# A float32 transformer block on one core: seven products for eight in the output projection's first two strips and in gate and up groups 0, 9 and 10, and the fourth merged quarter transposed by block exchange

## The chip, the core and the metric

The kernel runs on one core of a Trainium2 chip. The metric is the device time of one execution in microseconds. The core's engines are TensorE (PE, matmuls), VectorE (DVE), ScalarE (ACT), GpSimd (POOL) and SyncE (SP, which only issues DMAs); each works through its own instructions in a fixed order and waits where it needs another's result.

## The reference

One transformer block on 256 rows of 2048 numbers in float32. Three mixers (sparse attention, state space, retention) read one input projection; their outputs are merged, and what this case is about follows:

```python
    merged = g_nsa * (y_nsa @ p_nsa) + g_ssd * (y_ssd @ p_ssd) + g_ret * (y_ret @ p_ret)
    return merged @ w_out
...
    x = x + mix.astype(x.dtype)
    f = rms_norm(x, norm_ffn[l])
    x = x + ((jax.nn.silu(f @ w_gate[l]) * (f @ w_up[l])) @ w_down[l]).astype(x.dtype)
return rms_norm(x, norm_final)
```

`w_out` is 2048 x 2048, `w_gate` and `w_up` are 2048 x 5632, `w_down` is 5632 x 2048.

## The kernel before

**A product.** Each float32 number is split into a high part (fp32r, made by ACT: `wh`, `mh`, `fh`) and the rest (made by DVE as number minus high part: `wl`, `ml`, `fl`). A product of a 128x128 block of activations with a 128x512 block of weights is three matmuls into one PSUM bank: high x high, high x low, low x high. The 256 rows are two row tiles t. Activations are kept transposed, features on partitions, in 16 blocks of 128 (`mh`, `ml` for merged, `fh`, `fl` for the normalized x2); four blocks are a quarter.

**stream()** multiplies by one strip of 512 weight columns. For each pair of feature blocks it loads a 512 KB tile `raw` (SP's queue), makes `wh` and `wl` of it (rings of four), and issues four products, 12 matmuls. **stream_pair()** takes two strips at once, in eight steps j of two feature blocks each. A plain j is 8 products, 24 matmuls, into four banks c11 to c22. A fast j adds and subtracts blocks of the weights on DVE, needs ready-made sums of activation blocks (X, from `block_sums()`), and does 7 products, 21 matmuls, some into the four further banks m1, m5, m6, m7, which `capture()` adds into the result at the end of the last fast j. Which j are fast, and the order of the steps, are lists given by the caller.

**The stages around the change.** `merge_pair()` makes the two halves of merged. Its quarters 0, 1 and 2 are transposed into `mh`, `ml` by `task_exchange()`: DVE transposes 32x32 blocks into `tq`, 16 DMAs on POOL's queue move them to `st_x`, ACT makes the high part, DVE the low one. There is one `st_x` buffer at a time, so an exchange's DMAs wait until the one before has been read. Quarter 3 goes through 8 PE transposes into banks `hv` instead. Then four strips of `w_out` follow in stream(); `ev_o` adds half of each to x2, which `open_x2()` has loaded with x by four POOL DMAs. Behind each strip `task_f` transposes that quarter of x2 into `fh`, `fl` (quarters f0, f1, f2 by exchange with four scalings, f3 by 8 PE transposes `tf`). Then come 11 groups of one gate and one up strip, each a stream_pair. In groups 1 to 8 j=0 and 1 are fast, groups 0, 9 and 10 are plain. During them x2 lies in DRAM (`res`), its space holding sums and raw tiles; four POOL DMAs bring it back before group 10. The down projection adds the last product.

**What sets the order.** Tasks are generators in queues (`urgent` and others), of which a step is taken every third matmul; a queue is emptied at fixed places (`drain`). From that a scheduler makes each engine's order, with a high priority for weight loads and splits. A POOL DMA waits for the DMA eight before it on the queue.

Of the kernel before, what the change touches and what calls it, by code (L numbers as in the profile page):

```python
# [121 lines left out]
def _build(tc, a):  # L122
# [45 lines left out]
    def aux(name="ax"):  # L168
        return xp.tile([P, 512], F32, tag="ax", name=name)
# [48 lines left out]
    def pause(n):  # L218
        for _ in range(n):
            yield  # L220
# [43 lines left out]

    def stream_pair(xh, xl, K, srcs, cps, mps, order, X, capture, evac, new_raw, new_half, fast, hooks={}, tail=0):
        names = ("c11", "c12", "c21", "c22")
        C = [cps.tile([P, 512], F32, tag="mp" if cps is mp else "ax", name=n) for n in names]
        M = [mps.tile([P, 512], F32, tag="mp" if mps is mp else "ax", name=n) for n in ("m1", "m5", "m6", "m7")] if fast else []  # L270
# [43 lines left out]
        for n, j in enumerate(order[:len(order) - tail]):  # L314
            with tc.high_priority(offset=3000):
                ra, rb = load(j, 0), load(j, 1)
                h1, l1 = tiles()
                if j in fast:
                    wsum(rb[:, 0], rb[:, 0], rb[:, 1])
                halves(h1, l1, ra)  # L320
                if j in fast:
                    wsum(ra[:, 0], ra[:, 0], rb[:, 0])
                    wsum(ra[:, 1], ra[:, 1], ra[:, 0])
                    h2, l2 = new_half()
                    halves(h2, l2, rb[:, 1])
# [24 lines left out]
            if n in hooks:  # L350
                hooks[n]()
            if n == len(order) - 4:
                drain(urgent)
        for c in range(2 if tail else 0):
            held = []
# [832 lines left out]
    ml = mtp.tile([P, KD, S], F32R, name="ml")  # L1188

    def task_merged(c):  # L1190
        if c < 3:
            yield from pause(2)
            yield from task_exchange(mtp, merged[:, :, c * 512:(c + 1) * 512], mh, ml, c * 4)
            return
        yield from pause(6)
        for t in range(NT):
            ps = aux("hv")
            for b in range(4):
                transpose(ps[:, b * P:(b + 1) * P], merged[:, t, (4 * c + b) * P:(4 * c + b + 1) * P])
                yield  # L1200
            pv = ps.rearrange("p (b q) -> p b q", b=4)
            o = (slice(None), slice(4 * c, 4 * c + 4), slice(t * P, (t + 1) * P))
            act(mh[o], pv, AF.Copy)
            V.tensor_tensor(ml[o], pv, mh[o], OP.subtract)

    for c in (0, 2):
        merge_pair(2, yrh, yrl, 8, a["p_ret"], c, lambda c: urgent.append(task_merged(c)))
# [27 lines left out]
    for c in range(4):
        cs = slice(c * 512, (c + 1) * 512)

        def ev_o(t, ps):
            if c == 0 and t == 0:
                open_x2()  # L1240
            x2 = box["x2"]
            V.scalar_tensor_tensor(x2[:, t, cs], ps, 0.5, x2[:, t, cs], OP.mult, OP.add)
            jk = box["tmp"].tile([P, 512], F32, tag="jk", name="jk", bufs=3)
            act(jk, x2[:, t, cs], AF.Square, accum_out=sq2[:, t, c:c + 1])
        stream(mh, ml, KD, a["w_out"], c * 512, 512, ev_o)
# [26 lines left out]
    flip = [0]  # L1272

    def group(i):
        fast = GF if 1 <= i <= 8 else []
        if i == 9:
            s9_es.close()
            late, box["late_es"] = pool("late")
            for x_, n in ((hh, "hh9"), (hl, "hl9")):
                x_.late = late.tile([P, 4, S], F32R, name=n)  # L1280
        hb = tmp_p.tile([P, NT, 512], F32, tag="hb", name="hb", bufs=2)
        src = {}

# [110 lines left out]
    for c in (0, 2):  # L1394
        def capture(m1, m5, m6, m7):
            x = [[x2[:, t, (c + n) * 512:(c + n + 1) * 512] for n in range(2)] for t in range(NT)]
            u, f = (tmp_p.tile([P, 512], F32, tag="jk", name=n, bufs=3) for n in ("u", "m5s"))
            act(u, m1, AF.Copy)
            act(f, m5, AF.Copy)
            V.tensor_tensor(x[0][0], x[0][0], m1, OP.add)  # L1400
            V.tensor_tensor(u, u, m6, OP.add)
            V.tensor_tensor(x[0][1], x[0][1], f, OP.add)
            V.tensor_tensor(x[0][1], x[0][1], u, OP.subtract)
            V.tensor_tensor(u, u, m7, OP.add)
            V.tensor_tensor(x[1][0], x[1][0], u, OP.add)
# [9 lines left out]
        order = spread(4, std, fast, 4) if c == 0 else spread(1, std, fast, 3)  # L1415
# [34 lines left out]
```

## Time and profile before

| | |
|---|---|
| median of 3 runs (lowest, highest) | 1791.72 us (1791.63, 1792.75) |
| the profiled execution: its time, its span | 1790.73 us, 1789.0 us |
| TensorE busy | 1775.5 us, 99% |
| VectorE, ScalarE, GpSimd busy | 73%, 51%, 14% |
| chain that ended last | PE 96%, issue 2%, DVE 1% |

The span is what the profiler saw between the first and the last instruction; the execution's own time is 1.73 us longer. "Busy" of PE counts pipelined matmuls, so 99% means that it seldom waits.

### The profile page before, as it was taken

How to read it: one execution, taken by the hardware profiler on the slowest of the kernel's cores; microseconds unless marked ns; L12 is line 12 of the kernel's file. 1: busy time of each engine (PE TensorE's matmuls, PEld its weight loads, DVE VectorE, ACT ScalarE, POOL GpSimd, SP SyncE). 2: the span in 40 equal slices, each digit the busy share in tenths (PEclk: the TensorE clock that was granted, in tenths of full speed). 3: DMA queues.
4: the chain of work that ended last, by engine and by line, in shares of the span. 5: the costliest groups of instructions: out<-in, count | busy, mean ns of one | idle time of the engine just before them, and what ended most of it. 6: DMA issues, size and time to landing. Idle time of an engine off the chain costs nothing.

```text
span 1789.0 us, 22765 instructions
## 1 busy us (share of the span) xinstructions
PE 1775.5 (99%) x8220; PEld 1476.3 (83%) x8220; DVE 1304.8 (73%) x1613; ACT 920.6 (51%) x1170; POOL 242.6 (14%) x447
## 2 busy tenths in 40 slices
PE   9999999999999999999999999999999999999997
PEld 8878888988888888888888788888888888888886
DVE  7698986656664446577777665989998885777876
ACT  7465554546554444445445444555555554454543
POOL 0002222000000001310132430111112221100000
PEclk9999999999999999999999999999999999999999
DMA  9366555864555654656566886666666676676663
GB/s 354 118 213 200 188 169 162 264 201 153 162 166 166 200 186 156 221 191 212 186 202 214 267 262 224 199 222 212 204 210 203 206 241 209 200 228 211 198 211 118
DMA packets 196993, 362.52 MB, mean 203 GB/s; under 512 B 17056, under 2 KB 31648, under 8 KB 196368
## 3 DMA queue, kind: packets, MB, share of 16 engines
q1 hardware_dynamic: 181760, 335.65, 58.6%
q0 software_dynamic: 14688, 24.72, 4.1%
q8 instruction: 64, 1.05, 0.2%
q10 hardware_dynamic: 432, 0.70, 0.1%
q14 instruction: 49, 0.40, 0.1%
HBM read 344.71 MB, written 4.23 MB: 195 GB/s over the span
## 4 chain that ended last, share of the span: by engine, by line
PE 96%; issue 2%; DVE 1%; DMA 0%; ACT 0%; POOL 0%; POOLq 0%; DVEq 0%; ACTq 0%
PE mp L251 42%; PE c L288 41%; PE m L288 5%; PE hp L589 3%; PE yd L737 1%; PE c L859 0%; DMA erow<-adram 0%; PE pT L193 0%; DVE erow L696 0%; PE hp L564 0%; PE ny L811 0%; PE ny L807 0%; PE ny L809 0%; PE yo L742 0%; DVE wl L239 0%
## 5 line engine op out<-in xcount | busy, mean ns | idle before, releaser
L155 ACT ACTIVATE wh<-raw 128x1024 fp32r<-128x1024 f32 (+2 forms) x568 | 593.1, 1048 | 606.2 <-PE mp L251 305.4
L239 DVE TENSOR_TENSOR wl<-raw,wh 128x1024 fp32r<-128x1024 f32 (+2 forms) x304 | 365.9, 1207 | 227.5 <-ACT wh L155 224.5
L300 DVE TENSOR_TENSOR wl<-raw,wh 128x1024 fp32r<-128x1024 f32 x264 | 321.4, 1225 | 140.2 <-ACT wh L155 135.9
L251 PE MATMUL mp<-wl,uh 128*128 128x512 f32 (+2 forms) x832 | 319.1, 384 | 1.5 <-DVE wl L239 1.5
L251 PE MATMUL mp<-wh,ul 128*128 128x512 f32 (+2 forms) x832 | 319.7, 385 | 0.0
L251 PE MATMUL mp<-wh,uh 128*128 128x512 f32 (+2 forms) x832 | 317.8, 391 | 0.0
L449 POOL DMA_DIRECT2D st_x<-tq x368 | 182.6, 503 | 459.1 <-DVE tq L446 396.3
L288 PE MATMUL c<-wl,fh 128*128 128x512 f32 x608 | 236.7, 389 | 0.0
L288 PE MATMUL c<-wh,fl 128*128 128x512 f32 x608 | 236.5, 389 | 0.0
L288 PE MATMUL c<-wh,fh 128*128 128x512 f32 x608 | 226.4, 390 | 0.0
L251 PEld LDWEIGHTS mp<-wh,ul 128*128 128x128 f32 x832 | 156.4, 188 | 29.9 <-issue 0.2
L251 PEld LDWEIGHTS mp<-wh,uh 128*128 128x128 f32 x832 | 155.6, 188 | 30.6
L251 PEld LDWEIGHTS mp<-wl,uh 128*128 128x128 f32 x832 | 156.6, 188 | 29.1 <-DVE wl L239 1.9
L155 ACT ACTIVATE wh<-x 128x1024 fp32r<-128x1024 f32 x80 | 84.8, 1060 | 122.5 <-PE c L288 65.4
L288 PEld LDWEIGHTS c<-wh,fh 128*128 128x128 f32 x608 | 114.0, 188 | 24.2 <-ACT wh L155 0.4
L288 PEld LDWEIGHTS c<-wl,fh 128*128 128x128 f32 x608 | 114.1, 188 | 23.8 <-DVE wl L300 0.4
L288 PEld LDWEIGHTS c<-wh,fl 128*128 128x128 f32 x608 | 114.1, 188 | 23.7
L300 DVE TENSOR_TENSOR wl<-x,wh 128x1024 fp32r<-128x1024 f32 x80 | 97.5, 1219 | 23.1 <-ACT wh L155 23.0
L288 PE MATMUL c<-wl,hh 128*128 128x512 f32 x292 | 113.6, 389 | 0.0
L288 PE MATMUL c<-wh,hl 128*128 128x512 f32 x292 | 113.6, 389 | 0.0
L288 PE MATMUL c<-wh,hh 128*128 128x512 f32 x292 | 108.1, 389 | 0.0
L288 PEld LDWEIGHTS c<-wh,hh 128*128 128x128 f32 x292 | 54.8, 188 | 11.4
(423 smaller groups left out, 2611.7 us busy)
## 6 DMA issues: line engine op xcount, KB each, us to landing
raw<-in_w_in_dram SPq DMA_DIRECT2D x240, 512.0 KB, 3.6
raw<-in_w_up_dram SPq DMA_DIRECT2D x88, 512.0 KB, 4.7
raw<-in_w_down_dram SPq DMA_DIRECT2D x88, 512.0 KB, 4.9
x<-in_w_gate_dram SPq DMA_DIRECT2D x64, 512.0 KB, 4.5
raw<-in_p_ssd_dram SPq DMA_DIRECT2D x32, 512.0 KB, 3.7
raw<-in_w_out_dram SPq DMA_DIRECT2D x32, 512.0 KB, 4.6
raw<-in_w_gate_dram SPq DMA_DIRECT2D x24, 512.0 KB, 4.5
st_x<-tq POOLq DMA_DIRECT2D x368, 32.0 KB, 3.8
```

The source lines that it names most:

```text
L155: return nc.scalar.activation(out, in_, func, **kw)
L239: V.tensor_tensor(wl[:, ks, :n], raw[:, ks, :n], wh[:, ks, :n], OP.subtract)
L251: mm = nc.tensor.matmul(o, xx[:, k, ts], ww[:, kk, :n], start=(k == 0 and i == 0), stop=(k == K - 1 and i == 2))
L288: mm = nc.tensor.matmul(bank[o], xx, ww, start=first and i == 0, stop=last and i == 2)
L300: behind("DVE", V.tensor_tensor(o, u, v, op))
L449: queue.dma_start(st[32 * b:32 * b + 32, x], tq[32 * x:32 * x + 32, b])
L589: nc.tensor.matmul(hps[c][t][:, 0:n], xx[:, k, ts], ww[:, c0:c0 + n], start=(k == 0 and i == 0), stop=(k == KD - 1 and i == 2))
L737: nc.tensor.matmul(ps[:, h * 64:(h + 1) * 64], erow[:, h, t, :], xdt[:, t, h * 64:(h + 1) * 64], start=True, stop=True)
```

## The change

1. The output projection's first two strips become one stream_pair with j=0 and 1 fast, in the order 2, 3, 0, 4, 5, 1, 6, 7. The activation sums XO are made by block_sums. `capture_o` adds half of the m banks straight into x2. x2 is loaded (`open_x2`) behind the fourth step. Strips 2 and 3 stay with stream(), in the other four banks. The f tasks of quarters 0 and 1 are both queued behind the pair.
2. Groups 0, 9 and 10 have j=0 and 1 fast too. Group 0 goes 2, 3, 4, 0, 5, 1, 6, 7 and makes the sums of `fh`, `fl` that group 1 made. Groups 9 and 10 use parts of x2's space for sums and raw tiles.
3. The fourth merged quarter goes through task_exchange like the others.
4. x2 comes back from DRAM behind group 10, not before it. The down projection's first pair spreads its fast steps by `spread(6, ...)`, not 4.

```diff
     def task_merged(c):
-        if c < 3:
-            yield from pause(2)
-            yield from task_exchange(mtp, merged[:, :, c * 512:(c + 1) * 512], mh, ml, c * 4)
-            return
-        yield from pause(6)
-        for t in range(NT):
-            ps = aux("hv")
-            for b in range(4):
-                transpose(ps[:, b * P:(b + 1) * P], merged[:, t, (4 * c + b) * P:(4 * c + b + 1) * P])
-                yield
...
-            act(mh[o], pv, AF.Copy)
-            V.tensor_tensor(ml[o], pv, mh[o], OP.subtract)
+        yield from pause(2)
+        yield from task_exchange(mtp, merged[:, :, c * 512:(c + 1) * 512], mh, ml, c * 4)
...
+    def half_more(x, v, s_=0.5):
+        V.scalar_tensor_tensor(x, v, s_, x, OP.mult, OP.add)
+
+    def capture_o(m1, m5, m6, m7):
+        x = [[box["x2"][:, t, n * 512:(n + 1) * 512] for n in range(2)] for t in range(NT)]
+        u, f = (box["tmp"].tile([P, 512], F32, tag="jk", name=n, bufs=3) for n in ("uo", "m5o"))
+        act(u, m1, AF.Copy)
+        act(f, m5, AF.Copy)
+        half_more(x[0][0], m1)
+        V.tensor_tensor(u, u, m6, OP.add)
+        half_more(x[0][1], f)
+        half_more(x[0][1], u, -0.5)
+        V.tensor_tensor(u, u, m7, OP.add)
+        half_more(x[1][0], u)
+        half_more(x[1][1], f)
+        half_more(x[1][1], u, -0.5)
+
+    XO = block_sums(mh, ml, 0, 2, mg["left"], *xs)
+    stream_pair(mh, ml, KD, [(a["w_out"], 0), (a["w_out"], 512)], mp, xp, [2, 3, 0, 4, 5, 1, 6, 7], XO, capture_o,
...
+                {3: open_x2}, drains=(2, 4))
+    for c in range(2):
+        urgent.append(task_f(c))
+    for c in range(2, 4):
+        stream(mh, ml, KD, a["w_out"], c * 512, 512, lambda t, ps: ev_o(c, t, ps), banks=xp)
         urgent.append(task_f(c))
...
     def group(i):
-        fast = GF if 1 <= i <= 8 else []
+        fast = GF
+        parts = sums if i < 9 else [x2[:, 0, n * 512:(n + 1) * 512] for n in range(4)]
...
         def half():
+            if i > 8:
+                return [hlp.tile([P, 2, 512], F32R, tag=t, name=t)[:, 0] for t in ("wh", "wl")]
...
-        order = std[:2] + fast[:1] + std[2:4] + fast[1:] + std[4:]
-        if i == 1:
+        order = std[:2] + fast[:1] + std[2:4] + fast[1:] + std[4:] if i else [2, 3, 4, 0, 5, 1, 6, 7]
+        if i == 0:
...
             XG.update(block_sums(fh, fl, 0, len(GF), tmp_p, *v))
```

On POOL's queue, around the output projection, the order was this before: the last addition into merged, the loads of x2 (`x2<-in_x_dram`), and then a write of one quarter of x2 to DRAM (`res`) ahead of each f quarter's sixteen exchange DMAs.

```order
L1076 TENSOR_TENSOR merged_2620<-merged_2620,gt_7813 128x512 x2
L1223 DMA x2_8516<-in_x_dram 128x2x512 x4
L1322 DMA res_9085<-x2_8516 256x1x512
L449 DMA st_x_8548<-tq_8547 32x256 x16
L1322 DMA res_9085<-x2_8516 256x1x512
L449 DMA st_x_8726<-tq_8725 32x256 x16
L1322 DMA res_9085<-x2_8516 256x1x512
L449 DMA st_x_8904<-tq_8903 32x256 x16
L1322 DMA res_9085<-x2_8516 256x1x512
```

And the same stretch of POOL's queue in the changed kernel:

```order
L1076 TENSOR_TENSOR merged_2620<-merged_2620,gt_7813 128x512 x2
L1211 DMA x2_8563<-in_x_dram 128x2x512 x4
L449 DMA st_x_8404<-tq_8403 32x256 x16
L1331 DMA res_9151<-x2_8563 256x1x512
L449 DMA st_x_8766<-tq_8765 32x256 x16
L1331 DMA res_9151<-x2_8563 256x1x512
L449 DMA st_x_8891<-tq_8890 32x256 x16
L1331 DMA res_9151<-x2_8563 256x1x512 x2
L449 DMA st_x_8970<-tq_8969 32x256 x16
```

The merged quarter's exchange (`st_x_8404`) now stands behind the loads of x2, and f2's exchange (`st_x_8970`) behind all four `res` writes, where it had three ahead of it.

On DVE, before, the third and the fourth merged quarter's low parts stood together in the first output strip, behind that strip's weight splits:

```order
L239 TENSOR_TENSOR wl_8476<-raw_8474,wh_8475 128x1024
L239 TENSOR_TENSOR wl_8494<-raw_8492,wh_8493 128x1024
L466 TENSOR_TENSOR ml_7299<-st_x_8264,mh_7298 128x4x8x32
L1204 TENSOR_TENSOR ml_7299<-hv_8385,mh_7298 128x4x128
L1204 TENSOR_TENSOR ml_7299<-hv_8410,mh_7298 128x4x128
```

In the changed kernel the fourth quarter's low part is this row on DVE, the last one, near the end of the output pair:

```order
L300 TENSOR_TENSOR wl_8705<-raw_8700,wh_8704 128x1024
L300 TENSOR_TENSOR wl_8709<-raw_8702,wh_8708 128x1024
L1230 SCALAR_TENSOR_TENSOR x2_8563<-m5o_8653,x2_8563 128x512 x2
L1230 SCALAR_TENSOR_TENSOR x2_8563<-uo_8652,x2_8563 128x512
L1241 TENSOR_TENSOR uo_8652<-uo_8652,m7_8381 128x512
L1230 SCALAR_TENSOR_TENSOR x2_8563<-uo_8652,x2_8563 128x512 x2
L466 TENSOR_TENSOR ml_7299<-st_x_8404,mh_7298 128x4x8x32
```

It has moved behind the last weight splits of the pair and behind six operations of `capture_o`.

On DVE in group 0 of the changed kernel, the scaling of f2 (L464) stands behind the block sums (`bs`, `hl` by L402) and the first fast step's weight sums:

```order
L411 TENSOR_TENSOR bs_9170<-bs_9170,bs_9171 128x256
L300 TENSOR_TENSOR raw_9311<-raw_9311 128x512
L300 TENSOR_TENSOR hl_9143<-raw_9313,hh_9142 128x512
L402 TENSOR_TENSOR hl_9143<-bs_9170,hh_9142 128x2x128
L300 TENSOR_TENSOR raw_9313<-raw_9311,raw_9313 128x512
L300 TENSOR_TENSOR wl_9326<-raw_9311,wh_9325 128x1024
L1259 TENSOR_SCALAR r2_8349<-r2_8349 128x2
L1260 TENSOR_TENSOR r2_8349<-r2_8349 128x2
L464 TENSOR_SCALAR st_x_8970<-st_x_8970,prm_76 128x4x64 x4
L466 TENSOR_TENSOR fl_8347<-st_x_8970,fh_8346 128x4x8x32
```

Before, that scaling was the fourth row behind the last output strip's additions to x2, with two weight splits of group 0 and none of the sums ahead of it.

On PE the fast step of group 0 meets f2 here (`wh_9279` is of step 4, whose activations are quarter f2):

```order
L288 MATMUL m1_9181<-wl_9316,fh_8346 128x512
L288 MATMUL m1_9181<-wh_9315,fl_8347 128x512
L288 MATMUL m6_9183<-wh_9325,hh_9142 128x512
L288 MATMUL m6_9183<-wl_9326,hh_9142 128x512
L288 MATMUL m6_9183<-wh_9325,hl_9143 128x512
L288 MATMUL c11_9177<-wh_9279,fh_8346 128x512
L288 MATMUL c11_9177<-wl_9280,fh_8346 128x512
L288 MATMUL c21_9179<-wh_9279,fh_8346 128x512
```

Before, step 4 was the fifth of the group; now it is the third, with one m1 and one m6 product of step 0 ahead of it.

## Rows read from the trace of the kernel before

**Rows 1.** The page's parts 1 and 4: busy time and the chain.

```profile
PE 1775.5 (99%) x8220; PEld 1476.3 (83%) x8220; DVE 1304.8 (73%) x1613; ACT 920.6 (51%) x1170; POOL 242.6 (14%) x447
...
PE 96%; issue 2%; DVE 1%; DMA 0%; ACT 0%; POOL 0%; POOLq 0%; DVEq 0%; ACTq 0%
```

**Rows 2.** The waits of PE, whole span: us in total, times, longest.

```profile
PE mp L251 <- DVE wl L239: 1.5, 1, 1.5
...
PE mp L251 <- ACT mh L155: 1.2, 1, 1.2
PE mp L251 <- DVE ml L466: 0.2, 1, 0.2
```

**Rows 3.** The chain that ended last, groups 2 and 3: start, us, what.

```profile
1181.16 10.43 PE c L288 x46
...
1196.35 21.76 PE c L288 x96
...
1223.32 10.43 PE c L288 x46
```

**Rows 4.** Stretches: length, busy us of PE, PEld, DVE, ACT, POOL; clock; DMA share; GB/s.

```profile
950.00:1000.00 50.00, 49.75 (x224) 41.08 (x222) 35.69 (x35) 25.41 (x28) 15.48 (x24) 1.00 0.67 213
1000.00:1050.00 50.00, 48.78 (x214) 40.06 (x215) 30.46 (x34) 23.22 (x29) 19.42 (x37) 1.00 0.85 277
1150.00:1200.00 50.00, 50.00 (x220) 40.95 (x219) 46.04 (x52) 29.12 (x33) 7.84 (x16) 1.00 0.70 224
1500.00:1550.00 50.00, 50.00 (x222) 41.40 (x221) 30.61 (x32) 23.20 (x24) 7.88 (x16) 1.00 0.65 205
1780.00:1785.00 5.00, 0.00 (x0) 0.00 (x0) 2.44 (x7) 1.63 (x5) 0.54 (x1) 0.85 0.86 286
```

**Rows 5.** PE's timeline around the hv transposes: start, us, operation, idle before.

```profile
998.72 1.03 PE L193 MATMUL hv<-cst,merged 128*128 128x128 f32 x8
1000.97 0.50 PE L251 MATMUL mp<-wh,mh 128*128 128x512 f32 x1 [1.22 <-ACT mh L155]
...
1002.42 0.74 PE L251 MATMUL mp<-wh,ml 128*128 128x512 f32 x2 [0.25 <-DVE ml L466]
```

**Rows 6.** DVE's timeline in group 1.

```profile
1133.15 0.69 DVE L300 TENSOR_TENSOR raw<-x,raw 128x512 f32<-128x512 f32 x1
1133.76 1.22 DVE L300 TENSOR_TENSOR wl<-x,wh 128x1024 fp32r<-128x1024 f32 x1
1134.89 0.42 DVE L411 TENSOR_TENSOR bs<-bs 128x256 f32<-128x256 f32 x1
1135.23 0.42 DVE L402 TENSOR_TENSOR hl<-bs,hh 128x256 fp32r<-128x256 f32 x1
```

**Rows 7.** POOL's timeline, the loads of x2.

```profile
1000.35 2.92 POOL L1223 DMA_DIRECT2D x<-in_x_dram  x4 [6.44 <-issue]
```

**Rows 8.** DMA issues from 1000 to 1003.5 us: count, size, median us to landing.

```profile
x<-in_x_dram POOLq DMA_DIRECT2D x4, 512.0 KB, 9.4
```

**Rows 9.** Tile st_x, whole span: DMA issue to landing.

```profile
DMA to landing us min/median/max: 1.6/3.8/6.9
```

**Rows 10.** Groups of instructions by form, 990 to 1160 us: xcount | busy us, mean ns.

```profile
L464 DVE TENSOR_SCALAR st_x<-st_x,prm 128x256 f32<-128x256 f32 x12 | 3.5, 347 | 0.2 <-issue 0.2
L155 ACT ACTIVATE fh<-st_x 128x1024 fp32r<-128x1024 f32 x3 | 3.2, 1056 | 0.4 <-DMA res<-x 0.4
```

**Rows 11.** POOL's timeline, exchanges of f1 and f2 and the last res write.

```profile
1039.57 4.43 POOL L449 DMA_DIRECT2D st_x<-tq  x9 [2.74 <-DVE fl L466]
...
1048.70 2.02 POOL L449 DMA_DIRECT2D st_x<-tq  x4 [0.38 <-DMA st_x<-tq]
...
1063.07 5.43 POOL L449 DMA_DIRECT2D st_x<-tq  x11 [5.01 <-DVE fl L466]
...
1070.64 1.48 POOL L449 DMA_DIRECT2D st_x<-tq  x3 [0.17 <-issue]
1079.12 0.71 POOL L1322 DMA_DIRECT2D res<-x  x1 [7.00 <-DVE x L1242]
```

More of the change, by code (lines that the diff above doesn't have):

```diff
@@ L263, in stream, with stream_pair @@
             evac(t, ps[t][:, :n])
-    def stream_pair(xh, xl, K, srcs, cps, mps, order, X, capture, evac, new_raw, new_half, fast, hooks={}, tail=0):
+    def stream_pair(xh, xl, K, srcs, cps, mps, order, X, capture, evac, new_raw, new_half, fast, hooks={}, tail=0, drains=()):
         names = ("c11", "c12", "c21", "c22")
@@ L351, in stream_pair @@
                 hooks[n]()
-            if n == len(order) - 4:
+            if n in (drains or (len(order) - 4,)):
                 drain(urgent)
@@ L1190, in task_merged @@
     def task_merged(c):
-        if c < 3:
-            yield from pause(2)
-            yield from task_exchange(mtp, merged[:, :, c * 512:(c + 1) * 512], mh, ml, c * 4)
-            return
-        yield from pause(6)
-        for t in range(NT):
-            ps = aux("hv")
-            for b in range(4):
-                transpose(ps[:, b * P:(b + 1) * P], merged[:, t, (4 * c + b) * P:(4 * c + b + 1) * P])
-                yield
-            pv = ps.rearrange("p (b q) -> p b q", b=4)
-            o = (slice(None), slice(4 * c, 4 * c + 4), slice(t * P, (t + 1) * P))
-            act(mh[o], pv, AF.Copy)
-            V.tensor_tensor(ml[o], pv, mh[o], OP.subtract)
+        yield from pause(2)
+        yield from task_exchange(mtp, merged[:, :, c * 512:(c + 1) * 512], mh, ml, c * 4)
     for c in (0, 2):
@@ L1233, in task_f, with ev_o @@
             yield from to_features(box["x2"], c * 512, R("nffn"), c * 4, fh, fl, c * 4)
[L1235 to L1245, printed above, removed]
+    def ev_o(c, t, ps):
+        xv = box["x2"][:, t, c * 512:(c + 1) * 512]
+        V.scalar_tensor_tensor(xv, ps, 0.5, xv, OP.mult, OP.add)
+        jk = box["tmp"].tile([P, 512], F32, tag="jk", name="jk", bufs=3)
+        act(jk, xv, AF.Square, accum_out=sq2[:, t, c:c + 1])
+    def half_more(x, v, s_=0.5):
[15 more added lines that the diff above has]
+    stream_pair(mh, ml, KD, [(a["w_out"], 0), (a["w_out"], 512)], mp, xp, [2, 3, 0, 4, 5, 1, 6, 7], XO, capture_o,
+                lambda t, n, ps: ev_o(n, t, ps), lambda: rawp.tile([P, 2, 512], F32, tag="raw", name="raw"),
+                lambda: [mg["left"].tile([P, 512], F32R, tag="lone" + n, name="lone" + n) for n in "hl"], [0, 1],
+                {3: open_x2}, drains=(2, 4))
[3 more added lines that the diff above has]
+        stream(mh, ml, KD, a["w_out"], c * 512, 512, lambda t, ps: ev_o(c, t, ps), banks=xp)
         urgent.append(task_f(c))
@@ L1297, in raws @@
             box["n"] = n = box.get("n", 0) + 1
-            if 1 <= i <= 8 and n % 2:
-                t, c = divmod(n // 2 % 4, 2)
+            if i >= 1 and n % 2:
+                t, c = divmod(n // 2 % 4, 2) if i < 9 else (1, n // 2 % 2)
                 return x2[:, t, c * 1024:(c + 1) * 1024].rearrange("p (k c) -> p k c", k=2)
@@ L1311, in group @@
         stream_pair(fh, fl, KD, [(a["w_gate"], i * 512), (a["w_up"], i * 512)], *((mp, xp) if i % 2 == 0 else (xp, mp)),
-                    order, XG, take_out(sums, src), ev, raws, half, fast)
+                    order, XG, take_out(parts, src), ev, raws, half, fast)
         urgent.append(task_hidden(hb, i))
     for i in range(11):
-        if i == 10:
-            for c in range(4):
-                nc.gpsimd.dma_start(x2[:, :, c * 512:(c + 1) * 512], res[:, :, c * 512:(c + 1) * 512])
         group(i)
@@ L1322, in _build @@
                 nc.gpsimd.dma_start(res[:, :, c * 512:(c + 1) * 512], x2[:, :, c * 512:(c + 1) * 512])
+    for c in range(4):
+        nc.gpsimd.dma_start(x2[:, :, c * 512:(c + 1) * 512], res[:, :, c * 512:(c + 1) * 512])
     X = {}
@@ L1414, in _build @@
         std = [j for j in range(KF // 2) if j not in fast]
-        order = spread(4, std, fast, 4) if c == 0 else spread(1, std, fast, 3)
+        order = spread(6, std, fast, 4) if c == 0 else spread(1, std, fast, 3)
         stream_pair(hh, hl, KF, [(a["w_down"], c * 512), (a["w_down"], c * 512 + 512)], *((xp, mp) if c == 0 else (mp, xp)),
```

## The prediction

> **What bounds the kernel now.** The page comes first: TensorE (PE) is busy 99% of the span, and the chain that ended last is PE for 96% [rows 1]. So a matmul taken away is worth its time, unless PE then waits for what it multiplies. The waits of PE come next: the longest in the whole span is 1.5 us, for a `wl`, and two, 1.2 us for `mh` and 0.2 us for `ml`, lie in the stretch that the change rewrites [rows 2]. There is hardly a wait to win, then, and much room for new ones. The chain gives the price of a product: 96 matmuls of 128x512 follow each other in 21.76 us, 0.2267 us each, three to a product. A group of today's fast kind returns every 42.16 us (1181.16 to 1223.32), where 192 matmuls would take 43.52 us [rows 3]: the 1.36 us are the two products saved, six matmuls. In the trace, then, the trick gives its arithmetic back in full where VectorE (DVE) keeps up. Whether it does there is read from the windows: DVE is busy 46.0 of 50 us in a stretch of fast groups (1150 to 1200), 30.6 of 50 in plain group 10 (1500 to 1550), 30.5 of 50 in the output projection (1000 to 1050) [rows 4]. The new fast pairs therefore have room on the mean; the question is the order at two places.
>
> I count from T, the output projection's first matmul (the transposes stand at 998.72, 48 matmuls behind it, so T = 998.72 - 10.88 = 987.8), and from G, the start of gate and up group 0.
>
> **What is removed.** The output pair and groups 0, 9 and 10 each lose two products: 4 x 6 x 0.2267 = 5.44 us on PE's path. The eight transposes of the fourth merged quarter (1.03 us) go, and with them the wait behind them: 1000.97 for the next matmul, less 998.72 and 1.03, is 1.22 us, and 0.25 us follows for `ml` [rows 5]. That is 2.50 us, all of it PE time. Together -7.94 us.
>
> **The fourth quarter's new way.** It is wanted only when PE reaches pair j=6, behind four plain and two fast j: 4 x 24 x 0.2267 + 2 x 21 x 0.2267 = T+31.3. On POOL the four loads of `x2` stand ahead of its sixteen DMAs. I walk DVE's order with the starts of [rows 6] (a 128x1024 one 1.13 us after the last, a 128x512 one 0.61, a 128x256 one 0.34): the two transposes `tq` come at T+13.2 to 14.5. Then four loads issue in 2.92 us [rows 7], to T+17.5, and land 9.4 us after issue [rows 8], at T+24 to T+26.9. Four of the sixteen issue behind them, the next four each wait for a load's landing (the program lets a POOL DMA wait for the one eight back, as the wait for `st_x` in [rows 11] shows), the last ones for those; the last issues at about T+30.5, lands 3.8 us later [rows 9] at T+34.2, and ACT's `mh` takes 1.05 us [rows 10]: T+35.2. From T+31.3 PE waits 3.9 us. It then has eight matmuls that want `mh` alone (1.8 us) before it wants `ml`.
>
> `ml` is later. In DVE's order two `wl` and six 512-wide operations of `capture_o` stand ahead of it. The banks m5 and m7 end with the last fast product, at T+31.3; `wl_8705` starts at about T+31.5, then 2 x 1.13 + 6 x 0.61 + 1.2 = 7.2 us, `ml` at T+38.7. Without any wait PE would want it at T+31.3 + 1.8 = 33.1, so both waits together cost **5.6 us**. Bounds: if the two `wl` run earlier, the six operations and `ml` still follow the banks and ACT's copy of m5 (0.6 us): T+36.7, and `mh` and the eight matmuls need T+37; so 3.9 us. If the loads land 5 us later, `ml` is at about T+41.5, 8.4 us. `ml` of the third quarter, whose transposes and DMAs all lie ahead, has no such queue: eight matmuls cover it, nothing added.
>
> **The third f quarter.** Before, quarter f2's exchange ended at 1072 (1070.64 + 1.48), before group 0 began near 1077.6, and its first use was pair j=4, behind four others. Now f0 and f1 are queued behind the pair, so f1 runs in the last strip, and f2 waits in POOL's order for `fl` of f1 (one `st_x` buffer), which DVE makes behind the last strip's two x2 additions: G+2.05 (one and a half of these, 0.8, and 1.2). Sixteen DMAs took 9.05 us for f2 and 11.15 us for f1 in the trace [rows 11]; with 3.8 us landing and less 0.5 for the last issue, f2 is in by G+14.4 to G+16.5. The last output strip's `res` write goes ahead of it; it took 0.71 us before and costs nothing against the wait for `fl`.
>
> DVE is later still. Between `fl` of f1 and f2's scaling it has 5 `wl` (5.7), five 512-wide (3.0) and fourteen 256-wide operations (4.8, the block sums of `fh`, `fl`, which were in group 1 with seven pairs of cover), four `fl` from `tf` (1.6): 15.1 us, G+17.2. Then the scaling, four at 0.35, and ACT's `fh`, 1.05 [rows 10]: G+19.6, with ACT's queue about G+19.8. PE's order now has pairs 2 and 3, the eight `tf` transposes, one m1 and one m6 product, then j=4: 54 x 0.2267 + 1.03 = G+13.3. The wait is **6.5 us**, in two or three pieces (m6 itself wants `wl_9326`, near G+17.2, the last of that list). Bounds: were DVE free, 14.4 + 1.4 + 1.05 = G+16.9, 3.6 us; with a landing of 6.9 us (the maximum of [rows 9]) behind the slower sixteen, 19.6 + 2.45 = G+22.1, 8.8 us.
>
> **The rest, at nothing.** The block sums of `mh`, `ml` (14 small operations) lie in the merge pair before T, where DVE was busy 35.7 of 50 us (950 to 1000) [rows 4]; uncovered they would cost 14 x 0.34 = 4.8 us. Groups 9 and 10 get five more DVE operations per fast j, 3 us twice in 42 us, on an engine with 19 idle in 50 [rows 4]; their lone half takes a whole buffer of four, so an ACT or DVE tile may be late by up to 1 us a fast j, 4 us in all at worst; by the walk it isn't. The late reload of `x2` (four loads at 0.73 us, the landing of [rows 8] as an upper bound) is due on DVE only some 26 us into the down projection; `spread(6, ...)` is what moves that need.
>
> **Sum.** -5.44 - 2.50 + 5.6 + 6.5 = +4.2 us. The profiled execution took 1790.73 us, so 1794.9; the median of the runs shown is 0.99 above it, 1791.72, so **1795.9 us**.
>
> **Rivals.**
> *Clean gain* (the other side): DVE takes the exchanges before its queue. Then only the -7.94 stands: 1783.8 us. For it: the fast groups of today run without a PE wait [rows 2, 3]. Against: their X sums and features are complete a group earlier, and DVE runs its list in order. It decides at T+33.1 for `ml` and G+13.3 for `fh`; each us by which one is later costs one, and below 7.9 in sum the change gains, below 4.3 by more than can be mistaken.
> *One wait only or both near the lower bounds*: 3.9 + 3.6 - 7.94 = -0.4, or one wait alone of 5.6 or 6.5, -2.3 or -1.4: 1789.4 to 1791.3, no change that can be told. For it: DVE's list was walked with the starts of a busy stretch, and any of it that is done earlier shortens the wait behind it.
> *The clock falls in the waits.* In the trace the wait of 1.2 us left the granted clock at 1.00 (1000 to 1050), and the only drop is behind the last matmul, 0.85 for 1780 to 1785 [rows 4], where PE does nothing; of the two levels, 1.2 and 2.4 GHz, that is some of each. A wait of 3.9 us is not in the trace. If eight matmuls behind each of two long waits ran at half rate, 2 x 8 x 0.2267 = 3.6 us more: 1799.5 us; a whole pair j behind each, 10.9. The Trainium skill, in "TensorE: Matmul & The Clock Gate", Part 1, says that "the default state is throttled, and activity releases the throttle", and that idleness returns to it; by that rule the waits would cost this on top. The drop at the end of the trace agrees, the wait of 1.2 us shows nothing of it.
> *More waits*: the reload or the whole-buffer halves of groups 9 and 10 come late, 2 to 4 us on top, 1798 to 1800.
> *It doesn't do what it says* (the split products are arranged so that PE issues as many): the order shows 24 fewer matmuls and 8 fewer transposes, so this has next to no chance.
>
> **How the numbers follow.** Forecast, both waits about as sized, 1793 to 1798: 0.50. Clock or more waits, 1798 to 1803: 0.17. One wait or both small, 1788.5 to 1793: 0.20. Clean or nearly, 1783 to 1788: 0.13. The range 1789.3 to 1801 takes in the bounds (-7.94 + 7.5 gives 1791.3, -7.94 + 17.2 gives 1801.0) and leaves out the clean gain and the worst of the clock. The likeliest case's own range is 1793 to 1798. Within 0.2% (about what a measurement of this kernel can tell from no change) is 1788.1 to 1795.3. Slower takes the second case and six tenths of the first (0.47), faster the last and a little of the third (0.16), same the rest (0.37).
>
> **What would show it.** PE's list of waits should have `c <- ACT mh` near 4 us and `c <- DVE ml` near 1.7 us some 31 to 39 us behind T, and in group 0 `m <- DVE wl` and `c <- ACT fh`, 6.5 us together, with none of 1.2 us behind `hv`. DVE should run from G+2 to G+18 without idle time, and POOL's sixteen of f2 should begin near G+2. The period of group 9 or 10 should be 42.2 us. The prediction is wrong if `ml` of the fourth quarter ends before T+34, if f2's scaling starts before G+14, or if the granted clock drops in a stretch behind a wait; if PE waits in groups 9 or 10, the forecast is too low.

## The result, and the profile after

| | before | changed |
|---|---|---|
| median (lowest, highest) | 1792.16 us (1791.63, 1792.75; 4 runs) | 1806.63 us (1806.38, 1806.78; 4 runs) |
| ratio, 95% interval | | 1.0081 [1.0063, 1.0098] |
| the profiled execution, its span | 1790.73 us, 1789.0 us | 1806.78 us, 1805.0 us |

The change costs 14.5 us in the medians; 4.2 were forecast, and 1801 was the range's end. The places were the right ones. The waits of PE in the changed kernel from the output projection on (us in total, times, longest), where before had the two for `mh` and `ml` of [rows 2]:

```profile
PE c L288 <- ACT mh L155: 6.3, 1, 6.3
PE m L288 <- ACT wh L155: 3.2, 2, 2.6
PE c L288 <- ACT fh L155: 2.5, 1, 2.5
PE m L288 <- DVE wl L300: 1.8, 3, 0.7
...
PE c L288 <- DVE ml L466: 1.0, 1, 1.0
```

The stretches, in the columns of [rows 4]. The granted clock is 0.86 and 0.90 here, where [rows 4] has 1.00 everywhere but at the end:

```profile
1000.00:1050.00 50.00, 41.27 (x160) 31.90 (x159) 36.06 (x42) 22.62 (x30) 16.46 (x31) 0.86 0.69 226
1100.00:1150.00 50.00, 43.52 (x178) 34.40 (x177) 38.49 (x53) 21.76 (x25) 6.97 (x3) 0.90 0.54 171
```

In the profiled executions the 16.0 us of span split like this. T is at 988.8, 0.9 us later than before; these 0.9 are there by 352 us, ahead of anything that the change touches. From T to the third strip's first matmul (1045.10) it is 56.3 us, where the two strips, `hv` and its waits took 43.52 + 2.50 = 46.0: +10.3. From there to the run of 46 matmuls in group 1 (1157.96; before it stood 42.16 us ahead of the one at 1181.16 [rows 3], at 1139.0) it is 112.9 us instead of 105.1: +7.8. Groups 9 and 10 give 2.7 back, and 0.3 us less is left over that I can't place.

**The output pair.** PE's timeline (start, us, operation, idle before):

```profile
1028.94 0.80 PE L288 MATMUL c<-wh,mh 128*128 128x512 f32 x1 [6.26 <-ACT mh L155]
...
1033.76 1.22 PE L288 MATMUL c<-wh,ml 128*128 128x512 f32 x2 [1.04 <-DVE ml L466]
1034.78 0.63 PE L288 MATMUL c<-wh,mh 128*128 128x512 f32 x1
1035.21 0.63 PE L288 MATMUL c<-wl,mh 128*128 128x512 f32 x1
...
1038.75 0.39 PE L288 MATMUL c<-wh,ml 128*128 128x512 f32 x1
1038.98 0.39 PE L288 MATMUL c<-wh,mh 128*128 128x512 f32 x1
...
1045.10 0.39 PE L251 MATMUL mp<-wh,mh 128*128 128x512 f32 x1
```

PE's last matmul of the second fast step ended at 1022.7, so it was at j=6 at T+33.9 (T+31.3 forecast), got `mh` at 1028.9 and `ml` at 1033.8 = T+45.0 (T+38.7 forecast). From 1034.78 to 1035.21 a matmul takes 0.43 us, from 1038.75 to 1038.98 it takes 0.23 again. The clock in stretches of 2 us says why (columns as before): it falls in the wait and is at half until 1038.

```profile
1024.00:1026.00 2.00, 0.00 (x0) 0.00 (x0) 1.48 (x3) 1.06 (x1) 0.00 (x0) 0.68 0.91 289
1034.00:1036.00 2.00, 2.00 (x5) 1.60 (x6) 0.00 (x0) 0.00 (x0) 0.00 (x0) 0.50 0.00 0
1038.00:1040.00 2.00, 2.00 (x9) 1.62 (x9) 1.23 (x1) 0.79 (x2) 0.00 (x0) 0.91 0.00 0
```

What `mh` and `ml` stood behind is in the timelines of ACT, first, and of DVE:

```profile
1026.40 1.06 ACT L155 ACTIVATE wh<-raw 128x1024 fp32r<-128x1024 f32 x1 [1.15 <-DMA raw<-in_w_out_dram]
1027.37 0.58 ACT L155 ACTIVATE m5o<-m 128x512 f32<-128x512 f32 x1
1027.85 1.05 ACT L155 ACTIVATE mh<-st_x 128x1024 fp32r<-128x1024 f32 x1
```

```profile
1014.25 0.69 DVE L300 TENSOR_TENSOR raw<-raw 128x512 f32<-128x512 f32 x1 [5.27 <-DMA raw<-in_w_out_dram]
...
1027.49 1.23 DVE L300 TENSOR_TENSOR wl<-raw,wh 128x1024 fp32r<-128x1024 f32 x1 [0.98 <-ACT wh L155]
...
1032.49 1.22 DVE L466 TENSOR_TENSOR ml<-st_x,mh 128x1024 fp32r<-128x1024 f32 x1
```

DVE waited 5.3 us for the weights of the second fast step (1014.25). ACT's split at 1026.40 belongs to the last step, j=7; it waited for weights, and m5's copy and `mh` stood behind it. The second of DVE's two `wl` ahead of `capture_o`, the one at 1027.49, was due near T+32.6 and came at T+38.7. What SP's queue waited for from 1000 to 1040 us (us in total, times, longest):

```profile
SPq L308 <- DVE wl L300: 26.1, 8, 10.6
```

The three weight loads that SP issued between 1004 and 1010 us, beside the loads of x2, took 9.4 to 11.1 us to land. Those issued in the same stretch took 5.5 to 6.4 us in e4 (experiment 3), where the loads are moved away, and 5.8 to 7.2 in the kernel before, where they were in flight, too. The two loads of j=7 were not slow, they landed in 4.1 and 5.0 us; but SP could issue them only at 1020.0 and 1021.3, after the wait of 10.6 us, when DVE's late splits had freed a `raw` buffer (there are four). On POOL stand the loads of x2 and what waited for them:

```profile
1003.94 2.92 POOL L1211 DMA_DIRECT2D x<-in_x_dram  x4 [8.96 <-DVE tq L446]
...
1017.94 4.41 POOL L449 DMA_DIRECT2D st_x<-tq  x9 [1.99 <-DMA x<-in_x_dram]
```

**Group 0.** The timelines of PE, DVE and POOL, one below the other:

```profile
1088.62 0.39 PE L288 MATMUL c<-wh,fh 128*128 128x512 f32 x1
...
1101.45 0.50 PE L288 MATMUL m<-wl,fh 128*128 128x512 f32 x1 [0.65 <-DVE wl L300]
...
1104.83 0.80 PE L288 MATMUL m<-wh,hh 128*128 128x512 f32 x1 [2.65 <-ACT wh L155]
1106.33 0.80 PE L288 MATMUL m<-wl,hh 128*128 128x512 f32 x1 [0.71 <-DVE wl L300]
...
1110.03 0.79 PE L288 MATMUL c<-wh,fh 128*128 128x512 f32 x1 [2.48 <-ACT fh L155]
```

```profile
1105.06 1.22 DVE L300 TENSOR_TENSOR wl<-raw,wh 128x1024 fp32r<-128x1024 f32 x1
1107.17 0.17 DVE L1259 TENSOR_SCALAR r<-r 128x2 f32<-128x2 f32 x1 [0.89 <-POOL r L198]
...
1107.75 1.14 DVE L464 TENSOR_SCALAR st_x<-st_x,prm 128x256 f32<-128x256 f32 x4 [0.22 <-issue]
```

```profile
1091.04 4.08 POOL L449 DMA_DIRECT2D st_x<-tq  x8 [0.42 <-DVE fl L466]
...
1100.52 5.81 POOL L197 TENSOR_SCALAR r<-r 128x2 f32<-128x2 f32 x1
```

PE stopped for `wl` and `wh` of the first fast step and then for `fh` of f2, 6.5 us in four waits (0.65, 2.65, 0.71, 2.48). f2's scaling, at 1107.75, stood behind two small operations on r2, for the first of which DVE waited 0.9 us on POOL. POOL's own on r, 128x2 numbers, lasted 5.8 us.

### The profile page after: what moved, and what is told of

Same layout as the page of the kernel before. It is cut to its first block, busy times and chain, and to the rows that moved or that the text cites. A ratio compares the mean times of both kernels' runs of the same rounds, so it can differ in the third digit from the quotient of the medians.

```text
span 1805.0 us, 22864 instructions
## 1 busy us (share of the span) xinstructions
PE 1777.2 (98%) x8188; PEld 1474.6 (82%) x8188; DVE 1362.5 (75%) x1708; ACT 938.7 (52%) x1197; POOL 256.0 (14%) x463
## 3 DMA queue, kind: packets, MB, share of 16 engines
q8 instruction: 64, 1.05, 0.2%
## 4 chain that ended last, share of the span: by engine, by line
PE 90%; DMA 3%; DVE 3%; issue 3%; ACT 1%; POOL 1%; SPq 0%; DVEq 0%; POOLq 0%; ACTq 0%
PE c L288 40%; PE mp L251 38%; PE m L288 6%; PE hp L589 3%; DMA raw<-in_w_out_dram 1%; PE yd L737 1%; DMA craw<-in_cmp_v_w_dram 1%; DVE wl L300 0%; ACT wh L155 0%; DMA erow<-adram 0%; POOL r L197 0%; DVE wl L239 0%; PE pT L193 0%; DMA st_x<-tq 0%; DVE erow L696 0%
## 5 line engine op out<-in xcount | busy, mean ns | idle before, releaser
L155 ACT ACTIVATE wh<-raw 128x1024 fp32r<-128x1024 f32 (+2 forms) x560 | 583.4, 1046 | 562.2 <-PE mp L251 279.1
L239 DVE TENSOR_TENSOR wl<-raw,wh 128x1024 fp32r<-128x1024 f32 (+2 forms) x288 | 344.3, 1199 | 212.3 <-ACT wh L155 211.4
L300 DVE TENSOR_TENSOR wl<-raw,wh 128x1024 fp32r<-128x1024 f32 (+1 forms) x272 | 332.6, 1231 | 95.3 <-ACT wh L155 90.4
L449 POOL DMA_DIRECT2D st_x<-tq x384 | 190.4, 503 | 459.4 <-DVE tq L446 379.7
L288 PE MATMUL c<-wl,fh 128*128 128x512 f32 x572 | 223.4, 391 | 0.0
L288 PE MATMUL c<-wh,fl 128*128 128x512 f32 x572 | 221.7, 389 | 0.0
L288 PE MATMUL c<-wh,fh 128*128 128x512 f32 x572 | 209.4, 391 | 2.5 <-ACT fh L155 2.5
L155 ACT ACTIVATE wh<-x 128x1024 fp32r<-128x1024 f32 x100 | 106.1, 1061 | 160.4 <-PE c L288 76.9
L251 PEld LDWEIGHTS mp<-wh,uh 128*128 128x128 f32 x832 | 155.6, 188 | 30.5
L251 PEld LDWEIGHTS mp<-wl,uh 128*128 128x128 f32 x832 | 156.6, 188 | 29.2 <-DVE wl L239 1.9
L300 DVE TENSOR_TENSOR wl<-x,wh 128x1024 fp32r<-128x1024 f32 x100 | 121.9, 1219 | 30.4 <-ACT wh L155 30.3
L300 DVE TENSOR_TENSOR raw<-raw 128x512 f32<-128x512 f32 x88 | 62.8, 714 | 10.6 <-DMA raw<-in_w_out_dram 5.3
```

What stands on the lines that cost most here:

```text
L155: return nc.scalar.activation(out, in_, func, **kw)
L239: V.tensor_tensor(wl[:, ks, :n], raw[:, ks, :n], wh[:, ks, :n], OP.subtract)
L251: mm = nc.tensor.matmul(o, xx[:, k, ts], ww[:, kk, :n], start=(k == 0 and i == 0), stop=(k == K - 1 and i == 2))
L288: mm = nc.tensor.matmul(bank[o], xx, ww, start=first and i == 0, stop=last and i == 2)
L300: behind("DVE", V.tensor_tensor(o, u, v, op))
L449: queue.dma_start(st[32 * b:32 * b + 32, x], tq[32 * x:32 * x + 32, b])
```

## Experiments

Each ratio is to the kernel before on the same chip, with its 95% interval. "Pair" is the time from T to the third strip in the profiled execution: 56.3 us in the changed kernel, 42.2 if PE never waited.

**1. The tail alone (e1_tail).** The kernel before with these lines of the change:

```diff
-        fast = GF if 1 <= i <= 8 else []
+        fast = GF if i else []
...
-        order = spread(4, std, fast, 4) if c == 0 else spread(1, std, fast, 3)
+        order = spread(6, std, fast, 4) if c == 0 else spread(1, std, fast, 3)
```

> The kernel before, with j=0 and 1 fast in groups 9 and 10 too, the late reload of x2 and spread(6, ...); output projection, fourth merged quarter and group 0 as before. If these parts are clean, as the rest of the trace of the changed kernel suggests (two groups of 42.16 instead of 43.52 us and no wait behind them), the time falls by 2.7 us, to about 1789.5 against 1792.2. Rival: the reload or the halves from the ring cost something that the other stalls hid: no change, 1792.

0.9986 [0.9977, 0.9995], 2.5 us faster. Groups 9 and 10, the late reload and the halves from the ring are as good as their products.

**2. Group 0 plain (e2_g0plain).**

```diff
-        fast = GF
+        fast = GF if i else []
...
-        order = std[:2] + fast[:1] + std[2:4] + fast[1:] + std[4:] if i else [2, 3, 4, 0, 5, 1, 6, 7]
-        if i == 0:
+        order = std[:2] + fast[:1] + std[2:4] + fast[1:] + std[4:]
+        if i == 1:
```

> The changed kernel with group 0 plain again (order 0 to 7, block sums in group 1). Theory: the waits of group 0 (6.5 us) and its matmuls at half clock (2.8 us) come from the early need of f2 and the block sums ahead of it, so they go, and 1.36 us of products comes back: 1806.6 - 7.9 = 1798.7. Rival: the f exchanges are late by themselves since f0 and f1 wait for the pair, and a plain group 0 still waits for f2: 1803 to 1805.

1.0037 [1.0023, 1.0051], 7.9 us below the changed kernel's ratio, and no wait for `fh` is left. The pair is as bad as ever (56.6 us).

**3. The loads of x2 behind the exchange (e4_x2behind).**

```diff
         for c in range(4):
-            nc.gpsimd.dma_start(box["x2"][:, :, c * 512:(c + 1) * 512], xres[:, :, c * 512:(c + 1) * 512])
+            ld = nc.gpsimd.dma_start(box["x2"][:, :, c * 512:(c + 1) * 512], xres[:, :, c * 512:(c + 1) * 512])
+            tc.add_manual_dep(ld.ins, last_st[0].ins.name, ..., reason="behind the exchange")
```

> The changed kernel with the four loads of x2 held behind the fourth merged quarter's sixteen DMAs on POOL (the low part of that quarter then also comes ahead of capture_o on DVE). Theory A, the loads ahead of the exchange make mh and the weights of the second fast step late: the waits of the output pair (some 9.5 us) and its half clock (2.3 us and more) nearly go, with up to 2 us back where capture_o now waits for x2: about 1796. Theory B, DVE's long list is what binds whatever the loads do: only some 3 us go, 1803.

1.0068 [1.0054, 1.0081], 2.3 us below the changed kernel's ratio: near theory B's number, but not for its reason. The pair took 53.1 us, the waits in the second fast step are gone, and the wait for `mh` is longer, 8.6 us. ACT's timeline:

```profile
1028.21 1.06 ACT L155 ACTIVATE wh<-raw 128x1024 fp32r<-128x1024 f32 x1 [4.64 <-DMA raw<-in_w_out_dram]
...
1029.65 1.05 ACT L155 ACTIVATE mh<-st_x 128x1024 fp32r<-128x1024 f32 x1
```

The sixteen DMAs were issued by 1018.5, but ACT stood at the last step's split until 1028.21, since its weights were now in flight together with the four loads. Both theories had left out that ACT and DVE take this split ahead of `mh` and `ml`.

**4. Two of the loads behind it (e5_x2half).** As 3, for `c >= 2` alone.

> The changed kernel with two of the four loads of x2 ahead of the fourth merged quarter's DMAs and two behind them; DVE's order stays (ml behind capture_o). Theory A (transfers): the second fast step's weights land some 4 us earlier and four DMAs wait for a load no more, so mh comes 4 to 5 us earlier and the time falls by 4 to 6 us, to 1801 to 1803. Theory B (DVE's list): ml still ends behind the same six operations, but these start when the second fast step ends, 1 to 2 us earlier: 1805.

1.0094 [1.0080, 1.0108]: no gain, neither theory. The pair took 58.1 us. ACT again:

```profile
1027.75 1.06 ACT L155 ACTIVATE wh<-raw 128x1024 fp32r<-128x1024 f32 x1 [3.62 <-DMA raw<-in_w_out_dram]
1029.57 1.06 ACT L155 ACTIVATE wh<-raw 128x1024 fp32r<-128x1024 f32 x1 [0.76 <-DMA raw<-in_w_out_dram]
```

Two splits stand ahead of `mh` there, and their weights landed at 1027.75 and 1029.57. Moving the exchange among the loads did not by itself bring `mh` earlier.

**5. mh and ml ahead of the last step's splits (e7_pin).** As 3, and

```diff
+            if n == pin:
+                for k in ("ACT", "DVE"):
+                    queued[k] = last_x[k].ins.name
...
-                {3: open_x2}, drains=(2, 4))
+                {3: open_x2}, drains=(2, 4), pin=7)
```

(`behind()` then holds the splits of the eighth step behind the exchange's `mh` and `ml`.)

> As e4_x2behind, and on ACT and DVE the weight splits of the output pair's last step are held behind mh and ml of the fourth quarter. Theory Q (the order of the queues): in e4 the sixteen DMAs were in by about 1022 and mh came at 1029.7 only because ACT stood at a split whose weights landed at 1028.2; now mh comes near 1023, PE's wait for it falls from 8.6 to about 1.5 us with no half clock behind it, and the last step waits 1 to 2 us for its weights: 7.5 us off e4, to 1.0026 of before. Theory W (weights): the last step's weights are what is late, PE waits there instead of at mh, and only 2 to 3 us go: 1.0054.

1.0028 [1.0016, 1.0040], theory Q to 0.4 us. The pair took 44.4 us. `mh` no longer stands behind the last step's first split, whose weights landed just ahead of 1026.98. ACT's timeline, and below it all waits of PE from 980 to 1150 us:

```profile
1024.98 1.05 ACT L155 ACTIVATE mh<-st_x 128x1024 fp32r<-128x1024 f32 x1
1026.98 1.06 ACT L155 ACTIVATE wh<-raw 128x1024 fp32r<-128x1024 f32 x1 [0.95 <-DMA raw<-in_w_out_dram]
```

```profile
PE tf L193 <- DVE x L1233: 2.5, 2, 1.3
PE m L288 <- ACT wh L155: 2.1, 1, 2.1
PE c L288 <- ACT mh L155: 1.6, 1, 1.6
PE c L288 <- ACT fh L155: 0.9, 1, 0.9
PE m L288 <- DVE wl L300: 0.8, 1, 0.8
PE c L288 <- DVE fl L472: 0.2, 1, 0.2
```

The wait for `mh` is 1.6 us, and it left the clock at 1.00. The waits of the transposes `tf` lie between the fourth strip and group 0 (1082.5 and 1084.1), for DVE's additions of that strip into x2. The other four rows are of group 0, where the granted clock still fell to 0.50. Holding the splits back with the loads of x2 left where they were was not run, so this shows what the order is worth with the loads behind the exchange, and not what it is worth alone.

**6. The same with group 0 plain (e8_pin_g0plain).**

> e7_pin with group 0 plain as in e2_g0plain. If the two places are independent, another 7.9 us below e7_pin: by theory Q 3.2 us below the kernel before, 0.998; by theory W 1.001.

1.0000 [0.9991, 1.0010], 5.0 us below e7_pin instead of 7.9: the places are not independent. In e7 group 0 had cost less to begin with, 3.8 us in its three longer waits and not 6.5. And in this order DVE had f2's scaling behind a split of step 4's weights, and PE waited 2.5 us for `fh` in a plain group, too:

```profile
1102.20 1.23 DVE L300 TENSOR_TENSOR wl<-raw,wh 128x1024 fp32r<-128x1024 f32 x1 [1.50 <-ACT wh L155]
...
1103.92 1.14 DVE L470 TENSOR_SCALAR st_x<-st_x,prm 128x256 f32<-128x256 f32 x4 [0.22 <-issue]
```

**7. r2 behind f2 (e6_r2late).** The r2 operations held behind f2's low part (`last_ol`) on DVE:

```diff
-    V.tensor_scalar(r2[:, 1, :], r2[:, 0, :], 0.5, None, OP.mult)
+    r2s = V.tensor_scalar(r2[:, 1, :], r2[:, 0, :], 0.5, None, OP.mult)
+    tc.add_manual_dep(r2s.ins, last_ol[0].ins.name, ..., reason="behind f2")
```

> The changed kernel with the two small operations on r2 behind f2's low part on DVE, not ahead of f2's scaling. In the changed kernel they waited 0.9 us there for POOL's two operations on r2, the first of which took 5.8 us, and took some 0.5 us with what stood around them. If that is on the path, fh of f2 comes 1.4 us earlier and the time falls by as much, to 1.0073 of before instead of 1.0081; if f2's own transfers bind, nothing changes.

1.0067 [1.0050, 1.0084]. The wait for `fh` in the profile fell from 2.5 to 0.9 us, as expected; the times can't tell 1.4 us from nothing.

**8. The wait filled (e9_fill).**

```diff
                 if n == last_s:
                     capture(*M)
+                    for _ in range(fill):
+                        nc.tensor.matmul(bank["c11"], zero, xh[:, 0:2, :].rearrange("p k s -> p (k s)"), start=False, stop=False)
```

> The changed kernel with 40 matmuls of 128x512 with a zero 128x128 operand added into bank c11 behind the second fast step of the output pair; they add zero, take 9.1 us at full clock and fill the time in which PE waited for mh and ml. If the half clock behind the wait costs on top of it (ten matmuls behind ml at 0.43 instead of 0.23 us), the time falls by 2.1 us in spite of the 40 more matmuls, to 1.0069 of before, and the granted clock stays 1.00 there. If the half clock costs nothing, or the filling outlasts the wait, the time is the same or more: 1.0081 and above.

1.0072 [1.0057, 1.0087]: 1.6 us below the changed kernel, but the two intervals overlap. The trace tells it. PE's timeline (34 of the 40 added matmuls stand in its first row; the trace has four more of them further up), and a stretch in the columns of [rows 4]:

```profile
1023.07 8.09 PE L348 MATMUL c<-mh,zero 128*128 128x512 f32 x34
1031.76 0.50 PE L290 MATMUL c<-wh,mh 128*128 128x512 f32 x1 [0.60 <-ACT mh L155]
...
1035.02 0.73 PE L290 MATMUL c<-wh,ml 128*128 128x512 f32 x2 [1.15 <-DVE ml L470]
```

```profile
1020.00:1030.00 10.00, 10.00 (x45) 8.10 (x44) 7.58 (x9) 5.45 (x7) 4.41 (x9) 1.00 0.81 250
```

With 40 matmuls of zeros in it the pair stays at 1.00 throughout, `ml` comes no earlier than it did (T+45.8, T = 989.24), and the pair takes 55.0 us instead of 56.3. So the half clock behind the wait cost at least 1.3 us on top of it; the changed kernel's own rows give 2.3 (next section).

**9. Group 0 fast, all ahead of it as before (e3_g0).** e1_tail and the change's two lines for group 0.

> e1_tail (output projection and exchanges as before) with group 0 fast too, in the changed kernel's order 2, 3, 4, 0, 5, 1, 6, 7. Here f2's exchange is in before group 0 begins, so of the changed kernel's waits in group 0 only those for DVE's list of sums can stay. Theory F (f2's lateness is what costs there): about 1 us of waits, so e1_tail's 0.9986 less 1.36 us plus 1: 0.9984. Theory D (the block sums and the first fast step come too early for DVE): some 4 us of waits and 1 of half clock stay: 1.0006.

0.9979 [0.9970, 0.9988]: theory F. The one wait of group 0 that is left:

```profile
PE m L288 <- DVE wl L300: 0.5, 1, 0.5
```

Here the f quarters are in early, and PE reaches the first fast step at G+15.0 (1095.83, G = 1080.82), with products of step 4 ahead of it; in the changed kernel it was there at G+11.8.

**10. Another order in group 0 (e10_order).** The changed kernel with one list changed:

```diff
-... if i else [2, 3, 4, 0, 5, 1, 6, 7]
+... if i else [2, 3, 6, 7, 0, 4, 1, 5]
```

> The changed kernel with one list changed: group 0 goes 2, 3, 6, 7, 0, 4, 1, 5, so the first fast step and f2 are wanted 10.9 us later. DVE's list ended at 1107 and fh of f2 at 1110 where PE wanted them at 1102 and 1103; both theories of group 0 (f2 late, DVE's list) say that its waits and half clock go, 9.3 us: 1.0029 of before. If the quarter f3 (transposes in group 0) is late in its turn, only part of it goes: 1.005.

1.0028 [1.0019, 1.0037], 9.5 us below the changed kernel's ratio: the whole of what was expected. In group 0 (1090 to 1150 us) this is the only row of PE's waits:

```profile
PE m L288 <- ACT wh L155: 0.8, 2, 0.6
```

**11 and 12. A version that gains (e11_pin_order, e12_sp).** e7_pin with that order, and then with two of x2's loads moved to SP:

```diff
+    def load_x2(kq):
+        if c == 2 and kq in (4, 6):
+            q = slice((kq // 2) * 512, (kq // 2 + 1) * 512)
+            ld = nc.sync.dma_start(box["x2"][:, :, q], xres[:, :, q])
```

> e7_pin with group 0 in the order of e10_order: 5 us fewer waits and 2 us less half clock than e7_pin: 0.999 of before; 0.998 if the wait of the transposes tf (2.5 us in e7_pin) goes too.

> e11_pin_order with the loads of x2's third and fourth quarter taken from POOL's queue and put on SP's, between the weights of the third output strip, 512 KB each. If the burst of four loads is what makes the last weights of the pair and the first of that strip late (waits of 2.3 and 0.6 us for them in e7_pin), these go: 2.5 us below e11_pin_order, about 0.9975. If not, the same as e11_pin_order.

0.9985 [0.9976, 0.9994] and 0.9967 [0.9954, 0.9979]. The last is 5.9 us faster than the kernel before and the best of all, though its interval overlaps that of e11 by a little. In e11's trace the `tf` waits of e7 were still there, 1.4 and 1.2 us, and behind them the granted clock fell:

```profile
1084.00:1086.00 2.00, 2.00 (x6) 1.62 (x5) 2.00 (x7) 1.07 (x3) 1.28 (x3) 0.50 0.91 242
```

All of e12's waits of PE from 980 to 1150 us:

```profile
PE c L290 <- ACT mh L155: 1.6, 1, 1.6
PE mp L253 <- DVE wl L241: 0.8, 1, 0.8
PE m L290 <- ACT wh L155: 0.3, 1, 0.3
```

Its pair takes 44.8 us, its two strips 44.6 for 43.5. The reason in its expectation was partly mistaken: the 2.3 us for weights that I put into e7's strip are the early wait of [rows 2], at 114 us, ahead of all that changed (1.5 us there, 1.5 to 2.3 in later profiles). What went against e11 are the 2.6 us of `tf` and the half clock behind them; the 0.8 and 0.3 us came instead. Why moving the loads took the `tf` waits away was not followed up.

## Why the prediction was wrong

*What is removed* (-7.94) agrees with what the runs show, as far as they go: the tail gave 2.5 of 2.7 us by itself, and with most of the waits gone 5.9 of the 7.94 came out.

*The two places* were right, and so was the direction.

*The fourth quarter* was sized wrongly: 5.6 us forecast, 56.3 - 42.2 = 14.2 measured. Of the 8.6 missing, 6.3 are `ml` at T+45.0 and not T+38.7. The step that failed is "`wl_8705` starts at about T+31.5, then 2 x 1.13 + ...": I took the splits ahead of `ml` to have their weights. I had let the four loads of x2, 2 MB at once, delay the sixteen DMAs on POOL, and nothing else. In the trace they also delayed the weights on SP's queue, first those of the second fast step (5.3 us on DVE); the late splits then held the `raw` buffers, so those of the last step were issued late, and its splits stood ahead of `mh` on ACT and of `ml` on DVE. The sixteen DMAs were later than forecast, too: POOL waited for a load until 1017.94, T+29.2 (T+26.9 forecast), and issued the last at 1021.9, T+33.1 (T+30.5). e4 and e7 show loads and order apart: with the loads moved and the splits still ahead the pair took 53.1 us, with the splits behind `mh` and `ml` 44.4. `capture_o`'s six operations do stand ahead of `ml` (1028.64 to 1032.49, 3.8 us), as I wrote; but in e4, where `ml` stands ahead of them, it still came at T+41.5 (1030.73 + 1.23, T = 990.46), right behind a `wl` that waited for its weights.

The other 2.3 are the half clock: behind `ml`, 40 of the pair's 186 matmuls were left, 9.1 us at full clock, and took 1045.1 - 1033.8 = 11.3. The wait of 6.3 us came in one piece because `mh` and not only `ml` was late. The rival "the clock falls in the waits" was thus no rival but a part of the case; it had 3.6 us and a share of 0.17, and it cost 2.3 here and, with the refilling of PE behind four waits, some 3 in group 0 (9.3 lost there by e2, whose 7.9 come on top of the two products' 1.36, or 9.5 by e10; 6.5 of them waits). I had read the trace of before as open on it, since its longest wait was 1.5 us. The rule of the Trainium skill, "TensorE: Matmul & The Clock Gate", Part 1, that the lower level is the default and idleness leads back to it, holds in this trace: 0.68 at 1024 to 1026, 0.50 until 1038. With a wait of 3.9 us in the forecast, it belonged in the sum.

*f2* came out in its size, 6.5 us of waits forecast and 6.5 measured, from G+12.2 to G+21.4 (G = 1088.62; G+13.3 to G+19.8 forecast). That the two sums agree is luck: `fh` was 1.6 us later than forecast, and the five matmuls between the waits took 1.6 us longer than at full clock. Of the reason I gave, DVE's list of sums, the walk was right: the list ended at G+17.7 (G+17.2 forecast). But the list costs little by itself: with the f quarters early it cost 0.5 us in e3, and with PE's order changed 0.8 in e10. What costs is that PE wants the list's results and f2 before they are there. The step that I left out is POOL's r: sixteen DMAs, then two operations on r, then DVE's two, stood ahead of the scaling, which started at G+19.1; with DVE's two out of the way (e6) the wait for `fh` was 1.6 us shorter.

*The rest, at nothing*, held: neither e1 nor the changed kernel has a wait of PE in groups 9 and 10, and behind them there is one of 0.8 us in e1, none in the changed kernel.

*Clean gain* was refuted as it stood, but most of it is in reach: e12 has the same arithmetic, with the loads, the last step's splits and one list in another order.

Left open is what the 1.6 us for `mh` and the 0.8 us for weights that e12 still has would take to go. The first has its place in e12's trace: on ACT `mh` stands behind the copy of m5, which starts at 1023.35, when PE's last fast product has ended, and the two take 0.60 and 1.05 us. `mh` ahead of that copy was not run.

## What to carry to other kernels

When a load is moved next to a stream of weights, price it for every queue that it meets, not only for the one it stands on: here the 2 MB hurt most where splits that waited for their weights stood at the head of ACT's and DVE's queues, with the operand that PE wanted behind them. A long wait of PE costs more than its length: the one of 6.3 us was followed by 9 us of matmuls at half clock. Shorter ones went either way: the 1.6 us for `mh` in e7 left the clock at 1.00; the two for `tf` in e11 were followed by 0.50 (1084 to 1086 us); and behind the early wait at 114 us, 1.9 us in e1 and in e3, the granted clock was 0.50 (116 to 118 us) in e1 and 1.00 in e3. And before trading arithmetic for order, ask what the order would allow: moving the steps that want late data to the end gave back what group 0 had lost, 9.5 us.

## What was unexpected of the hardware

POOL's multiply-add on 128x2 numbers, 0.18 us before (at 1080.61), lasted 5.81 us, from 1100.52 to 1106.33, while DVE ran two-input operations without a gap until 1106.28. In e4, e5, e6 and e9, where DVE has the same list, it lasted 5.4 to 6.1 us; in e2, where it has not, 0.19. The other way round, a `wl` of DVE lasted 3.28 us at 992.79, against 1.22, beside POOL's additions into merged. The Trainium skill, "SBUF — State Buffer", "Who interferes with whom", says that a DVE instruction with two inputs in SBUF contends with a GpSimd instruction that reads SBUF, and calls the ports that the two share an exclusive lock. The trace agrees, and goes further: the small instruction waited for ten of DVE's, not for one. It is not always so: in e7 it took 0.27 us, at 1096.81, in the middle of such a run on DVE, and what let it through there is not shown.
